# Running sums of weight tiles in a Strassen-type feed-forward block: accumulating DMAs instead of VectorE subtractions

## The chip, the cores and the metric

The kernel runs on one core of a Trainium2 chip. The metric is device time of one execution in microseconds, smaller is better. Before the change it takes 2362.85 us (median of three runs, 2361.63 to 2367.12).

## What is computed

The reference is one layer of an encoder for two sequences of 256 tokens (512 columns in all), width 2048, everything in float32:

```python
h = h + concat(neighbourhood_attention(xn), gated_deltanet_bidir(xn)) @ w_out   # xn = rmsnorm(h) @ w_in
hn = rmsnorm(h, norm_ffn_w)
h = h + (silu(hn @ w_gate) * (hn @ w_up)) @ w_down      # 2048 -> 5632 -> 2048
y = rmsnorm(h, final_norm_w)
```

The change touches only `hn @ w_gate` and `hn @ w_up`, and the preparation of their moving operand.

## The kernel before, in words

**Precision.** TensorE multiplies in fp32r. Every float32 operand is split into a high part (ScalarE rounds it, line 123) and a low part (VectorE subtracts the high part from the operand, line 124), and one product is three matmuls: high by high, high by low, low by high. A 128x1024 weight tile thus costs one ScalarE instruction and one VectorE instruction before its last matmuls can start. High and low tiles have three buffers each (`w_split`, line 874), so splits can run at most three products ahead of TensorE.

**The gate and up blocks.** `block` (line 883) computes two 128-column strips of gate or up for all 512 columns. The contraction (2048 = 2 x 1024) and the columns (two halves of 256) and the strips make a 2x2 by 2x2 block product, done in Winograd's form of Strassen's scheme: seven products instead of eight. Each `product` (line 866) is 24 matmuls of 256 columns. The moving operands, seven combinations of the four quarters of the normalised residual (A11, A12, S4, A22, S1, S2, S3), are made once ahead of the stage (lines 844 to 857) and kept in SBUF. The weight side needs seven operands for each block: four raw 512 KB tiles (b11, b12, b21, b22, loaded from HBM on the SP queue, lines 888 to 893) and combinations of them, which VectorE makes in place (lines 905, 909, 915, 927). Evacuation of the seven products to the four output quarters is a handful of ScalarE copies and VectorE additions.

There are 22 pairs of one gate and one up block, 44 blocks in all, in the loop at the end of the stage. b11 and b12 have one buffer in the gate pool and one in the up pool, so the two kinds of block alternate between them; b21 and b22 share a ring of three buffers with the other weight loads.

**What orders the work.** TensorE's matmuls keep program order. On the other engines a scheduler lists the instructions by priority; splits are written under `tc.high_priority(offset=AHEAD)` (120) and loads under three times that, which puts them ahead of their place in the program. Each engine and each DMA-issuing queue then runs its list strictly in order, waiting on semaphores. DMAs are issued from SP (weight loads) and from POOL (stores of the residual, line 843; stores of each pair's activations to `s_act`, line 971; their reload, line 995).

After the stage, the activations are reloaded for the down projection (`load_act`, line 990), whose loads are plain 512 KB DMAs issued from POOL into a ring of two buffers.

Of the kernel before, what the change touches and what calls it, by code (L numbers as in the profile page):

```python
# [8 lines left out]
F32 = mybir.dt.float32  # L9
# [3 lines left out]
ALU = mybir.AluOpType  # L13
# [4 lines left out]
P = 128  # L18
# [5 lines left out]
L = 256  # L24
# [34 lines left out]
def hybrid_encoder(ctx: ExitStack, tc: tile.TileContext, xT, w_in, w_ba, w_out, w_gate,  # L59
                   w_up, w_down, nw_mix, nw_ffn, nw_fin, na_bias, conv_w, lane_par,  # L60
                   dn_nw, y):
    nc = tc.nc
    act = nc.scalar.activation
    tt = nc.vector.tensor_tensor
# [5 lines left out]
    def mm(*a, **k):  # L70
        pin(nc.tensor.matmul(*a, **k))  # L71
# [6 lines left out]
    wp = ctx.enter_context(tc.tile_pool(name="wp", bufs=2, side="left"))  # L78
# [41 lines left out]
    def split(hi, lo, src, scale=None):  # L120

        if scale is None:
            act(out=hi, in_=src, func=AF.Copy)  # L123
            tt(lo, src, r32(hi), ALU.subtract)  # L124
# [710 lines left out]
    A11, A12, S4, A22, S1, S2, S3 = range(7)  # L835
    for n, i in enumerate(pairs):
        j = i % 8
        ps = pg.tile([P, T], F32, tag="g", name="ps_g")
        hk = st.tile([P, T], F32, tag="hk", bufs=2, name="hk")
        nc.sync.dma_start(hk, s_h1[i])  # L840
        half_gemm(ps, w_out[i, 1], dns, True, True)
        tt(hk, hk, ps, ALU.add)
        nc.gpsimd.dma_start(s_h2[i], hk)
        w = nwf[:, i:i + 1]
        if i < 8:
            cmb = st.tile([P, 7, L], F32, tag="cmb", name="cmb")
            a21 = st.tile([P, L], F32, tag="a21", name="a21")
            act(out=cmb[:, A11], in_=hk[:, :L], func=AF.Copy, scale=w)
            act(out=a21, in_=hk[:, L:], func=AF.Copy, scale=w)
            tt(cmb[:, S3], cmb[:, A11], a21, ALU.subtract)  # L850
        else:
            act(out=cmb[:, A12], in_=hk[:, :L], func=AF.Copy, scale=w)
            act(out=cmb[:, A22], in_=hk[:, L:], func=AF.Copy, scale=w)
            tt(cmb[:, S1], a21, cmb[:, A22], ALU.add)
            tt(cmb[:, S2], cmb[:, S1], cmb[:, A11], ALU.subtract)
            tt(cmb[:, S4], cmb[:, A12], cmb[:, S2], ALU.subtract)
            split(XH[j], XL[j], cmb)
        sq = acc if n == 0 else st.tile([P, T], F32, tag="sq", name="h_sq")
        act(out=sq, in_=hk, func=AF.Square)
        if n:  # L860
            tt(acc, acc, sq, ALU.add)
# [4 lines left out]
    def product(ps, w, c, first, done=False):  # L866

        wh, wl = w
        for k in range(8):
            for n, (u, x) in enumerate(((wh, XH), (wh, XL), (wl, XH))):  # L870
                mm(ps, u[:, k], x[k][:, c], start=(first and k == 0 and n == 0),
                   stop=(done and k == 7 and n == 2), skip_group_check=True)

    def w_split(src):
        hi = wp.tile([P, 8, P], F32R, tag="hi", bufs=3, name="w_hi")
        lo = wp.tile([P, 8, P], F32R, tag="lo", bufs=3, name="w_lo")
        split(hi, lo, src)
        return hi, lo

    def ahead():  # L880
        return tc.high_priority(offset=AHEAD)

    def block(src, f, pool, new_out, opened=None):

        with tc.high_priority(offset=3 * AHEAD):
            b11 = pool.tile([P, 8, P], F32, tag="b11", name="b11")
            b12 = pool.tile([P, 8, P], F32, tag="b12", name="b12")
            nc.sync.dma_start(b11, src[f, 0])
            nc.sync.dma_start(b12, src[f + 1, 0])
            b22 = wp.tile([P, 8, P], F32, tag="raw", bufs=3, name="b22")  # L890
            nc.sync.dma_start(b22, src[f + 1, 1])
            b21 = wp.tile([P, 8, P], F32, tag="raw", bufs=3, name="b21")
            nc.sync.dma_start(b21, src[f, 1])
        pa = pg.tile([P, T], F32, tag="g", name="ps_a")
        pc = psm.tile([P, T], F32, tag="s", name="ps_c")
        with ahead():
            w = w_split(b11)
        product(pa[:, :L], w, A11, True)
        if opened:
            opened()  # L900
        fp, out = state["fp"], new_out()
        p1 = fp.tile([P, L], F32, tag="p1", bufs=2, name="p1")
        nc.scalar.copy(p1, pa[:, :L])
        with ahead():
            tt(b11, b12, b11, ALU.subtract)
            w = w_split(b11)
        product(pc[:, L:], w, S1, True)
        with ahead():
            tt(b12, b22, b12, ALU.subtract)
            w = w_split(b12)  # L910
        product(pc[:, :L], w, S3, False)
        p75 = fp.tile([P, 2, L], F32, tag="p75", bufs=2, name="p75")
        nc.scalar.copy(p75, pc.rearrange("p (a t) -> p a t", a=2))
        with ahead():
            tt(b11, b22, b11, ALU.subtract)
            w = w_split(b11)
        product(pa[:, L:], w, S2, False)
        u2 = fp.tile([P, L], F32, tag="u2", bufs=2, name="u2")
        tt(u2, p1, pa[:, L:], ALU.add)
        with ahead():  # L920
            w = w_split(b22)
        product(pc[:, L:], w, S4, False, True)
        v = fp.tile([P, L], F32, tag="v", name="v")
        tt(v, u2, p75[:, 0], ALU.add)
        tt(out[:, 3], v, p75[:, 1], ALU.add)
        with ahead():
            tt(b11, b21, b11, ALU.subtract)
            w = w_split(b11)
        product(pc[:, :L], w, A22, False, True)
        with ahead():  # L930
            w = w_split(b21)
        tt(out[:, 1:3], pc.rearrange("p (a t) -> p a t", a=2),
           u2[:, None, :].broadcast_to([P, 2, L]), ALU.add)
        product(pa[:, :L], w, A12, False, True)
        nc.scalar.copy(out[:, 0], pa[:, :L])
# [20 lines left out]
    for p in range(NPAIR):  # L956
        g4 = block(w_gate, 2 * p, gA,
                   lambda: state["fp"].tile([P, 4, L], F32, tag="g4", name="ga"),
                   open_gate if p == 0 else None)
        act(out=g4, in_=g4, func=AF.Silu)  # L960
        u4 = block(w_up, 2 * p, state["gB"],
                   lambda: state["fp"].tile([P, 4, L], F32, tag="u4", bufs=2, name="up"))
        tt(u4, u4, g4, ALU.mult)  # L963
        sA = state["sA"]
        if p // 2 == FIRST_SEG:
            k = p % 2 * 2
            split(sA[:, 0, k:k + 2].rearrange("p k t -> p (k t)"),
                  sA[:, 1, k:k + 2].rearrange("p k t -> p (k t)"),
                  u4.rearrange("p a t -> p (a t)"))
        else:  # L970
            nc.gpsimd.dma_start(s_act[p], u4.rearrange("p a t -> p (a t)"))  # L971
# [16 lines left out]
    fp = ctx.enter_context(tc.tile_pool(name="fq", bufs=2, side="left", reuse_waits="tile"))  # L988
# [174 lines left out]
```

## Time and profile before

| | |
|---|---|
| median of the runs | 2362.85 us |
| the profiled execution's own time | 2364.33 us |
| its span, first to last instruction | 2362.6 us |
| TensorE busy | 2323.2 us, 98% |
| VectorE busy | 1599.0 us, 68% |
| ScalarE busy | 975.0 us, 41% |
| mean granted TensorE clock | 0.996 |
| gate and up stage, first matmul to the last block's last copy | 965.5 to 1864.8 us |

A busy share is an average over stages with different limits. Matmuls overlap each other in the pipeline, so their busy times are added up from a modelled end; the distance between starts is the better measure. The rows of the stage are shown where the prediction uses them.

### The profile page before, as it was taken

To read this page: it belongs to the slowest core of one execution; us is meant where nothing else is said; L and a number is where in the kernel's file an instruction comes from. 1 tells how busy PE (TensorE), PEld (TensorE's weight loads), DVE (VectorE), ACT (ScalarE), POOL (GpSimd) and SP (SyncE) were. 2 spreads that over 40 slices of the span, in tenths; PEclk is the share of its full clock that TensorE was granted. 3 is DMA by queue.
4 is the path that set the end of the run, shared out by engine and by line. 5 is a ranking of instruction groups with operands and counts; after the bars stand their busy time and mean duration, and the time that the engine had idled before them with its cause. 6 is when DMAs were issued, how large, how long until landed. Compare 5 with 4: busy or idle time off the path is not lost.

```text
span 2362.6 us, 35608 instructions
## 1 busy us (share of the span) xinstructions
PE 2323.2 (98%) x14500; PEld 2058.6 (87%) x14500; DVE 1599.0 (68%) x2164; ACT 975.0 (41%) x1464; POOL 143.8 (6%) x244
## 2 busy tenths in 40 slices
PE   8999999999999999899999999999999999999997
PEld 6777788877778788799999999999999888888887
DVE  7644699985566637788888888888888653422346
ACT  6777223324333315544444444444444331211125
POOL 2111200002100001000000000000000110000000
PEclk9999999999999999999999999999999999999999
DMA  5434623346434546333333333333333563423332
GB/s 202 130 116 132 161 93 103 95 120 179 145 115 125 212 157 208 120 115 119 116 126 117 126 117 119 114 121 113 118 106 99 192 227 98 133 93 97 98 125 72
DMA packets 88980, 305.30 MB, mean 129 GB/s; under 512 B 11776, under 2 KB 16288, under 8 KB 87664
## 3 DMA queue, kind: packets, MB, share of 16 engines
q1 hardware_dynamic: 71392, 245.67, 32.5%
q0 software_dynamic: 17424, 57.36, 8.0%
q8 instruction: 114, 1.87, 0.3%
q14 instruction: 50, 0.41, 0.1%
HBM read 266.98 MB, written 36.00 MB: 128 GB/s over the span
## 4 chain that ended last, share of the span: by engine, by line
PE 57%; DVE 0%; DMA 0%; issue 0%; ACT 0%; POOL 0%; DVEq 0%
PE ps_c L71 21%; PE ps_a L71 16%; PE ps_g L71 11%; PE ps_s L71 9%; DMA raw_a<-s_act 0%; DVE hT L1043 0%; DVE w_lo L124 0%; DVE up L937 0%; ACT w_hi L123 0%; ACT aq L123 0%; DVE up L963 0%; DVE hT L1010 0%; DVE dgs L1037 0%; POOL s_act L971 0%; DVE ssq_acc L1060 0%
## 5 line engine op out<-in xcount | busy, mean ns | idle before, releaser
L123 ACT ACTIVATE w_hi<-b 128x1024 fp32r<-128x1024 f32 x308 | 327.0, 1062 | 490.9 <-PE ps_c L71 164.6
L124 DVE TENSOR_TENSOR w_lo<-w_raw,w_hi 128x1024 fp32r<-128x1024 f32 x224 | 274.1, 1224 | 277.9 <-ACT w_hi L123 273.9
L124 DVE TENSOR_TENSOR w_lo<-b,w_hi 128x1024 fp32r<-128x1024 f32 x308 | 376.3, 1222 | 120.3 <-ACT w_hi L123 120.3
L123 ACT ACTIVATE w_hi<-w_raw 128x1024 fp32r<-128x1024 f32 x224 | 236.8, 1058 | 487.0 <-PE ps_s L71 278.2
L71 PE MATMUL ps_c<-xch,w_hi 128*128 128x256 f32 x1408 | 399.9, 284 | 0.0
L71 PE MATMUL ps_c<-xcl,w_hi 128*128 128x256 f32 x1408 | 399.0, 283 | 0.0
L71 PE MATMUL ps_c<-xch,w_lo 128*128 128x256 f32 x1408 | 399.0, 283 | 0.0
L71 PE MATMUL ps_g<-xhi,w_hi 128*128 128x512 f32 x896 | 369.6, 412 | 0.0
L71 PE MATMUL ps_g<-xhi,w_lo 128*128 128x512 f32 x896 | 351.6, 392 | 6.6 <-DVE w_lo L124 6.6
L71 PE MATMUL ps_g<-xlo,w_hi 128*128 128x512 f32 x896 | 350.8, 392 | 0.0
L71 PE MATMUL ps_a<-xch,w_hi 128*128 128x256 f32 x1056 | 299.0, 283 | 5.3 <-ACT xch L123 4.0
L71 PE MATMUL ps_a<-xcl,w_hi 128*128 128x256 f32 x1056 | 299.1, 283 | 1.7 <-DVE xcl L124 1.7
L71 PE MATMUL ps_a<-xch,w_lo 128*128 128x256 f32 x1056 | 299.0, 283 | 0.0
L71 PEld LDWEIGHTS ps_c<-xch,w_hi 128*128 128x128 f32 x1408 | 271.0, 192 | 0.5 <-issue 0.5
L71 PEld LDWEIGHTS ps_c<-xcl,w_hi 128*128 128x128 f32 x1408 | 271.0, 192 | 0.5 <-issue 0.5
L71 PEld LDWEIGHTS ps_c<-xch,w_lo 128*128 128x128 f32 x1408 | 270.9, 192 | 0.0
L71 PEld LDWEIGHTS ps_g<-xhi,w_lo 128*128 128x128 f32 x896 | 168.8, 188 | 46.0 <-DVE w_lo L124 9.1
L71 PEld LDWEIGHTS ps_a<-xch,w_hi 128*128 128x128 f32 x1056 | 202.7, 192 | 5.7 <-ACT xch L123 4.2
L71 PEld LDWEIGHTS ps_g<-xhi,w_hi 128*128 128x128 f32 x896 | 169.0, 189 | 43.1 <-issue 7.4
L71 PEld LDWEIGHTS ps_a<-xcl,w_hi 128*128 128x128 f32 x1056 | 202.8, 192 | 1.9 <-DVE xcl L124 1.9
L71 PEld LDWEIGHTS ps_a<-xch,w_lo 128*128 128x128 f32 x1056 | 202.9, 192 | 0.0
L71 PEld LDWEIGHTS ps_g<-xlo,w_hi 128*128 128x128 f32 x896 | 169.3, 189 | 30.9 <-issue 0.2
(307 smaller groups left out, 3468.7 us busy)
## 6 DMA issues: line engine op xcount, KB each, us to landing
w_raw<-in_w_in_dram SPq DMA_DIRECT2D x112, 512.0 KB, 3.6
b<-in_w_gate_dram SPq DMA_DIRECT2D x88, 512.0 KB, 3.5
b<-in_w_up_dram SPq DMA_DIRECT2D x88, 512.0 KB, 3.5
w_raw<-in_w_down_dram SPq DMA_DIRECT2D x88, 512.0 KB, 3.5
w_raw<-in_w_out_dram SPq DMA_DIRECT2D x32, 512.0 KB, 3.6
s_act<-up POOLq DMA_DIRECT2D x20, 512.0 KB, 2.9
raw_a<-s_act POOLq DMA_DIRECT2D x20, 512.0 KB, 4.6
qg<-s_eg SPq DMA_DIRECT2D x8, 1024.0 KB, 4.6
```

The source lines that it names most:

```text
L71: pin(nc.tensor.matmul(*a, **k))
L123: act(out=hi, in_=src, func=AF.Copy)
L124: tt(lo, src, r32(hi), ALU.subtract)
```

## The change

The weight operands become running sums. Two tiles replace b11 and b12 (here B11, B12, B21, B22 are the four raw tiles):

- `second` is loaded with B12 and then receives B22 by an accumulating DMA; it is used once.
- `first` is loaded with B11, used, receives B12, is used again, receives B22, is used again, receives B21, and is used a last time. Each addition is a DMA of 512 KB from HBM with `accum_op=ALU.add`, issued from POOL, into the same SBUF buffer.

The four VectorE subtractions of a block go. Signs that they carried move to the combinations of the residual (lines 854 and 856: S1 becomes a difference, S4 a sum) and to the evacuation. The order of the seven products changes, and the evacuation with it: ScalarE copies p1, p7 and one output quarter; VectorE does d, u2, three output quarters one by one, and the scaling. Line numbers on the plus side are those of the changed kernel.

```diff
-            tt(cmb[:, S1], a21, cmb[:, A22], ALU.add)
+            tt(cmb[:, S1], a21, cmb[:, A22], ALU.subtract)
             tt(cmb[:, S2], cmb[:, S1], cmb[:, A11], ALU.subtract)
-            tt(cmb[:, S4], cmb[:, A12], cmb[:, S2], ALU.subtract)
+            tt(cmb[:, S4], cmb[:, A12], cmb[:, S2], ALU.add)
...
+    def plus(dst, src):
+        nc.gpsimd.dma_start(dst, src, accum_op=ALU.add)
...
         with tc.high_priority(offset=3 * AHEAD):
-            b11 = pool.tile([P, 8, P], F32, tag="b11", name="b11")
-            b12 = pool.tile([P, 8, P], F32, tag="b12", name="b12")
-            nc.sync.dma_start(b11, src[f, 0])
-            nc.sync.dma_start(b12, src[f + 1, 0])
+            first = pool.tile([P, 8, P], F32, tag="first", name="w_first")
+            nc.sync.dma_start(first, src[f, 0])
+            second = pool.tile([P, 8, P], F32, tag="second", name="w_second")
+            nc.sync.dma_start(second, src[f + 1, 0])
+            plus(second, src[f + 1, 1])
...
         with ahead():
-            w = w_split(b11)
+            w = w_split(first)
+            plus(first, src[f + 1, 0])
         product(pa[:, :L], w, A11, True)
...
         with ahead():
-            tt(b11, b12, b11, ALU.subtract)
-            w = w_split(b11)
-        product(pc[:, L:], w, S1, True)
+            w = w_split(second)
+        product(pc[:, :L], w, S3, True)
+        p7 = fp.tile([P, L], F32, tag="p7", bufs=2, name="p7")
+        nc.scalar.copy(p7, pc[:, :L])
         with ahead():
-            tt(b12, b22, b12, ALU.subtract)
-            w = w_split(b12)
-        product(pc[:, :L], w, S3, False)
-        p75 = fp.tile([P, 2, L], F32, tag="p75", bufs=2, name="p75")
-        nc.scalar.copy(p75, pc.rearrange("p (a t) -> p a t", a=2))
+            w = w_split(first)
+            plus(first, src[f + 1, 1])
+        product(pc[:, L:], w, S1, False)
+        d = fp.tile([P, L], F32, tag="d", bufs=2, name="d")
+        tt(d, pc[:, L:], p7, ALU.subtract)
         with ahead():
-            tt(b11, b22, b11, ALU.subtract)
-            w = w_split(b11)
-        product(pa[:, L:], w, S2, False)
+            w = w_split(b21)
+        product(pa[:, :L], w, A12, False)
+        nc.scalar.copy(out[:, 0], pa[:, :L])
+        with ahead():
+            w = w_split(first)
+            plus(first, src[f, 1])
+        product(pa[:, L:], w, S2, False, True)
         u2 = fp.tile([P, L], F32, tag="u2", bufs=2, name="u2")
         tt(u2, p1, pa[:, L:], ALU.add)
+        tt(out[:, 3], d, u2, ALU.subtract)
         with ahead():
             w = w_split(b22)
-        product(pc[:, L:], w, S4, False, True)
...
+        product(pc[:, L:], w, S4, False)
+        tt(out[:, 2], pc[:, L:], u2, ALU.subtract)
         with ahead():
-            tt(b11, b21, b11, ALU.subtract)
-            w = w_split(b11)
+            w = w_split(first)
         product(pc[:, :L], w, A22, False, True)
...
-        product(pa[:, :L], w, A12, False, True)
-        nc.scalar.copy(out[:, 0], pa[:, :L])
+        tt(out[:, 1], pc[:, :L], u2, ALU.add)
```

More of the change, by code (lines that the diff above doesn't have):

```diff
@@ L881, in ahead @@
         return tc.high_priority(offset=AHEAD)
+    def plus(dst, src):
+        nc.gpsimd.dma_start(dst, src, accum_op=ALU.add)
     def block(src, f, pool, new_out, opened=None):
         with tc.high_priority(offset=3 * AHEAD):
-            b11 = pool.tile([P, 8, P], F32, tag="b11", name="b11")
-            b12 = pool.tile([P, 8, P], F32, tag="b12", name="b12")
-            nc.sync.dma_start(b11, src[f, 0])
-            nc.sync.dma_start(b12, src[f + 1, 0])
+            first = pool.tile([P, 8, P], F32, tag="first", name="w_first")
[3 more added lines that the diff above has]
+            plus(second, src[f + 1, 1])
+            b21 = wp.tile([P, 8, P], F32, tag="raw", bufs=3, name="b21")
+            nc.sync.dma_start(b21, src[f, 1])
             b22 = wp.tile([P, 8, P], F32, tag="raw", bufs=3, name="b22")
             nc.sync.dma_start(b22, src[f + 1, 1])
-            b21 = wp.tile([P, 8, P], F32, tag="raw", bufs=3, name="b21")
-            nc.sync.dma_start(b21, src[f, 1])
         pa = pg.tile([P, T], F32, tag="g", name="ps_a")
@@ L904, in block @@
         with ahead():
-            tt(b11, b12, b11, ALU.subtract)
-            w = w_split(b11)
-        product(pc[:, L:], w, S1, True)
+            w = w_split(second)
+        product(pc[:, :L], w, S3, True)
+        p7 = fp.tile([P, L], F32, tag="p7", bufs=2, name="p7")
+        nc.scalar.copy(p7, pc[:, :L])
         with ahead():
-            tt(b12, b22, b12, ALU.subtract)
-            w = w_split(b12)
-        product(pc[:, :L], w, S3, False)
-        p75 = fp.tile([P, 2, L], F32, tag="p75", bufs=2, name="p75")
-        nc.scalar.copy(p75, pc.rearrange("p (a t) -> p a t", a=2))
-        with ahead():
-            tt(b11, b22, b11, ALU.subtract)
-            w = w_split(b11)
-        product(pa[:, L:], w, S2, False)
+            w = w_split(first)
[3 more added lines that the diff above has]
+        tt(d, pc[:, L:], p7, ALU.subtract)
+        with ahead():
+            w = w_split(b21)
[5 more added lines that the diff above has]
+        product(pa[:, L:], w, S2, False, True)
         u2 = fp.tile([P, L], F32, tag="u2", bufs=2, name="u2")
         tt(u2, p1, pa[:, L:], ALU.add)
+        tt(out[:, 3], d, u2, ALU.subtract)
         with ahead():
             w = w_split(b22)
-        product(pc[:, L:], w, S4, False, True)
-        v = fp.tile([P, L], F32, tag="v", name="v")
-        tt(v, u2, p75[:, 0], ALU.add)
-        tt(out[:, 3], v, p75[:, 1], ALU.add)
+        product(pc[:, L:], w, S4, False)
+        tt(out[:, 2], pc[:, L:], u2, ALU.subtract)
         with ahead():
-            tt(b11, b21, b11, ALU.subtract)
-            w = w_split(b11)
+            w = w_split(first)
         product(pc[:, :L], w, A22, False, True)
[L930 to L933, printed above, removed]
-        product(pa[:, :L], w, A12, False, True)
-        nc.scalar.copy(out[:, 0], pa[:, :L])
+        tt(out[:, 1], pc[:, :L], u2, ALU.add)
         a = out.rearrange("p (f b) t -> p f (b t)", f=2)
```

## Prediction

> **What bounds the kernel now.** I read the page first, then the stage that the change touches by stretches of time, then that stage's tiles and steps.
>
> ```profile
> span 2362.6 us, 35608 instructions
> ...
> PE 2323.2 (98%) x14500; PEld 2058.6 (87%) x14500; DVE 1599.0 (68%) x2164; ACT 975.0 (41%) x1464; POOL 143.8 (6%) x244
> ...
> DVE  7644699985566637788888888888888653422346
> ...
> PE 57%; DVE 0%; DMA 0%; issue 0%; ACT 0%; POOL 0%; DVEq 0%
> ```
>
> TensorE is busy 98% of the span, and the chain of work that ended last holds no VectorE time. VectorE's row stands at 7 and 8 tenths from slice 17 to slice 31, the gate and up stage. Within that stage, in busy us and instruction counts of each engine (PE, PEld, DVE, ACT, POOL), clock, DMA share and GB/s:
>
> ```profile
> 1100.00:1800.00 700.00, 700.00 (x5835) 700.00 (x5835) 575.06 (x576) 312.34 (x366) 8.53 (x16) 1.00 0.37 118
> ```
>
> TensorE and its weight loads are busy for all 700 us at full clock: 700/5835 = 0.120 us per matmul, 24 x 0.120 = 2.88 us per product. VectorE is at 82% and waits for others; it is not the limit. The tile ps_a gives the pace (minimum, median and maximum ns, first and last start):
>
> ```profile
> L71 PEld LDWEIGHTS ps_a<-xch,w_hi x1056: 186/192/192, 965.5 to 1863.3; 128*128 128x128 f32 x176
> L919 DVE TENSOR_TENSOR u<-p,ps_a x44: 420/422/422, 988.5 to 1855.3; 128x256 f32<-128x256 f32 x44
> L935 ACT COPY ga<-ps_a x22: 353/353/354, 998.0 to 1844.7; 128x256 f32<-128x256 f32 x22
> ```
>
> u is made once a block, so a block takes (1855.3 - 988.5)/43 = 20.16 us, which is 7 x 2.88. The first block takes 998.0 - 965.5 = 32.5 us because it waits for the moving operands. So the stage is TensorE's, and anything that shortens VectorE's list is worth nothing there unless TensorE has something to wait for.
>
> **What the change removes.** Groups of the stage by line, with busy us and mean ns:
>
> ```profile
> L927 DVE TENSOR_TENSOR b<-b,b 128x1024 f32<-128x1024 f32 x43 | 52.6, 1224 | 0.8
> L905 DVE TENSOR_TENSOR b<-b,b 128x1024 f32<-128x1024 f32 x42 | 51.5, 1226 | 1.4
> L915 DVE TENSOR_TENSOR b<-b,b 128x1024 f32<-128x1024 f32 x42 | 51.4, 1225 | 1.4
> L909 DVE TENSOR_TENSOR b<-b,b 128x1024 f32<-128x1024 f32 x42 | 51.1, 1216 | 0.0
> ```
>
> 44 x 4 = 176 VectorE instructions of 1.22 us go, 215 us of busy time, all beside a TensorE that never waits: worth 0 in the steady stage. The evacuation has one VectorE instruction more a block (d, u2, three quarters, scaling, against u2, v, two writes, scaling) and ScalarE as many as before: 0. The signs in the residual's combinations change no count: 0. The number of matmuls is the same: 0.
>
> **What it adds.** 176 accumulating DMAs of 512 KB, issued from POOL. Those into `second` have a block's time of lead and I cost them as traffic only. Those into `first` lie in a chain. The same buffer is split, added to, split, added to, split, added to, split: product 3's weights can't be copied by ScalarE before the addition has landed, the addition can't be issued before VectorE's low part of product 1 has read the tile, and so on. Three additions in a block. The next block has its own buffer, but the instruction order of the changed kernel puts its first split behind this block's last on both engines: on ScalarE the copies of products 7, 1', 2' (prime: next block) follow each other, on VectorE the low part of 7 is followed by u2, the out[:, 3] subtraction, and the low part of 1'. So the chains of consecutive blocks don't overlap. A block then takes
>
> P = 3 X + 3 S + E,
>
> if that is over 20.16, with X from the end of one low part to the start of ScalarE's copy of the sum, S from that start to the end of the next low part, and E from the low part of product 7 to that of product 1'. S and E come from steps in the timeline (start, duration):
>
> ```profile
> 1509.62 1.06 ACT L123 ACTIVATE w_hi<-b 128x1024 fp32r<-128x1024 f32 x1 [1.82 <-PE ps_c L71]
> ```
> ```profile
> 1510.72 1.23 DVE L124 TENSOR_TENSOR w_lo<-b,w_hi 128x1024 fp32r<-128x1024 f32 x1 [1.03 <-ACT w_hi L123]
> 1512.58 0.42 DVE L919 TENSOR_TENSOR u<-p,ps_a 128x256 f32<-128x256 f32 x1 [0.63 <-PE ps_a L71]
> 1513.10 0.43 DVE L924 TENSOR_TENSOR v<-u,p 128x256 f32<-128x256 f32 x1
> 1513.56 0.43 DVE L925 TENSOR_TENSOR ga<-v,p 128x256 f32<-128x256 f32 x1
> 1513.91 1.22 DVE L124 TENSOR_TENSOR w_lo<-b,w_hi 128x1024 fp32r<-128x1024 f32 x1
> 1516.43 1.23 DVE L124 TENSOR_TENSOR w_lo<-b,w_hi 128x1024 fp32r<-128x1024 f32 x1 [1.30 <-ACT w_hi L123]
> 1517.69 1.23 DVE L905 TENSOR_TENSOR b<-b,b 128x1024 f32<-128x1024 f32 x1
> ```
>
> S = 1510.72 + 1.23 - 1509.62 = 2.33. For E: a small instruction behind a low part starts about when that ends; then u2 to the next 0.52 (1513.10 - 1512.58), small to low part 0.35 (1513.91 - 1513.56), low part 1.22: 2.09. So P = 3 X + 6.99 + 2.09 = 3 X + 9.08, and it exceeds TensorE's 20.16 from X = 3.69 on.
>
> No row of before shows an accumulation. The nearest is the plain 512 KB load that POOL issues in the down stage, into a ring whose buffer VectorE's low part has just freed, and which ScalarE then waits for: the same loop.
>
> ```profile
> 1915.94 1.23 DVE L124 TENSOR_TENSOR ar<-raw_a,ar 128x1024 fp32r<-128x1024 f32 x1 [1.13 <-ACT ar L123]
> 1922.23 1.23 DVE L124 TENSOR_TENSOR ar<-raw_a,ar 128x1024 fp32r<-128x1024 f32 x1 [1.44 <-ACT ar L123]
> ```
> ```profile
> 1917.46 0.53 POOL L995 DMA_DIRECT2D raw_a<-s_act  x1 [2.42 <-DVE ar L124]
> 1923.76 0.53 POOL L995 DMA_DIRECT2D raw_a<-s_act  x1 [2.13 <-DVE ar L124]
> ```
> ```profile
> 1921.14 1.06 ACT L123 ACTIVATE ar<-raw_a 128x1024 fp32r<-128x1024 f32 x1 [1.60 <-DMA raw_a<-s_act]
> 1928.58 1.06 ACT L123 ACTIVATE ar<-raw_a 128x1024 fp32r<-128x1024 f32 x1 [1.90 <-DMA raw_a<-s_act]
> ```
> ```profile
> DMA to landing us min/median/max: 3.7/4.6/11.8
> ```
>
> X of a plain load: 1921.14 - 1917.17 = 3.97, and 1928.58 - 1923.46 = 5.12 in a stretch with other loads. The smallest landing, 3.7, and the 0.29 from VectorE's end to POOL's issue give 3.99 too. An accumulation also reads its destination. What 512 KB cost the engines, from 700 us of the stage:
>
> ```profile
> q1 hardware_dynamic: 20115, 73.29, 33.5%
> q0 software_dynamic: 2304, 8.39, 3.0%
> ...
> b<-in_w_gate_dram SPq DMA_DIRECT2D x71, 512.0 KB, 3.5
> b<-in_w_up_dram SPq DMA_DIRECT2D x69, 512.0 KB, 3.5
> s_act<-up POOLq DMA_DIRECT2D x16, 512.0 KB, 2.9
> ```
>
> 140 loads in 0.335 x 700 = 234.5 us of all 16 engines: 1.67 us each; a store 0.03 x 700/16 = 1.3. The second read adds between 0 (if it runs beside the first) and 1.67 (if behind it). I take 1.67, since the engine has to move twice the bytes in: X = 5.64 undisturbed. Then contention: a block's other traffic is four loads (6.7), the accumulation into `second` (3.3) and half a store (0.7), 10.7 us in a period near 28, 38%. An addition that meets a load may lose up to its 1.67; 0.38 x 1.67 = 0.65. I take X = 6.3; the ends are 3.97 (nothing for the second read, nothing met) and 5.12 + 2 x 1.67 = 8.46.
>
> On what only a page states: the Trainium skill, "Collectives: The Full Stack", section "The bandwidth ceiling", says that an addition in the DMA engine is free but takes two source reads on one ring, so that it moves at half a copy's rate. By that X would be 5.64 before contention and the time 2364 + 43 x (26.00 - 20.16) = 2615; no run so far shows an accumulation.
>
> **The sum.** P = 3 x 6.3 + 9.08 = 27.98, 7.82 us over 20.16. The first block's 32.5 us cover its own chain, so 43 blocks pay: 336 us. On the profiled execution's own 2364.33 (1.5 above the median of the runs): 2364 + 336 = 2700.
>
> **Waits and queues.** Behind ScalarE's waiting copy for product 3 stand the copy for 4, p1 and p7; none is needed before product 3 has run, so they add nothing. POOL holds the accumulation into the next same-kind `second` between the first and second addition to `first`; it waits for a load that SP issues after the low part of product 2, 1.57 us after that of product 1 (0.35 and 1.22), landing 3.5 us later: 5.1 us into the block. The second addition is ready at X + 2.33 = 8.6, later, so it isn't held; it would be only if that load were over 3 us late. SP's order of loads follows the splits that free their buffers, and each lands a block early. The `s_act` store stands ahead of the third addition and is ready by then. In the residual stage before, stores on POOL now stand behind the first accumulation into `second`: a few us at most, and in the first block three VectorE sums go ahead of the last moving operands, up to 3.7 us the other way. I cost both at 0.
>
> **The rivals.**
>
> - *The accumulation costs hardly more than a plain load.* X 3.97 to 5.1; for it speaks that the second read is from SBUF and might hide in the 2 us of a landing that isn't transfer (3.7 - 1.67); against it the doubled bytes. At X = 4.5: P = 22.58, 43 x 2.42 = 104, 2468 us.
> - *Every addition meets another transfer and queues.* The splits release loads and additions at the same moments, so the meetings aren't random: X 7.3 to 8.5. At 8.0: P = 33.08, 43 x 12.92 = 556, 2920 us. Against it: the DMA share is only 0.37 now.
> - *Not slower: the chain fits under TensorE.* The place is the loop above, and it decides at X = 3.69. Below that, TensorE stays the bound: 2364, or some 3.7 us less from the shorter first block, 2361. Against it: the smallest X seen for a plain load is 3.97. The Trainium skill, "DMA: Bandwidth & Descriptors", section "Anatomy of one DMA", gives 2.0 us plus the bytes at 436 GB/s, 3.2 us for 512 KB; by that X would be 3.5 and nothing would change. The trace disagrees, at 3.7 for the fastest of 20.
> - *The sums stay where they were.* The instruction order of the changed kernel has 176 more DMAs on POOL and 132 fewer instructions of two tensors on VectorE (176 sums less, 44 evacuations more), so this doesn't happen: chance 0.
>
> **How the numbers follow.** Forecast (X 5.1 to 7.3, 2546 to 2829): 0.53. Plain-like accumulation (X 3.73 to 5.1, up to 2546): 0.22. Queued accumulation (X over 7.3): 0.19. Fits under TensorE: 0.06, of which 0.02 faster. A measurement of this kernel tells 0.2%, some 4.7 us, from no change; the chain passes that at X = 3.73. So faster 0.02, same 0.04, slower 0.94. The range 2430 (X = 4.2) to 2950 (X = 8.24) leaves out the last case, a little of the plain-like case and half of the queued one, under 2 in 10.
>
> **What would show it.** Right: TensorE in the stage no longer at 100%, with three waits a block, ahead of products 3, 5 and 7, near 2, 3 and 3 us, released by the low part and behind it by the DMA into w_first; block period near 28; landing of these DMAs near 6 us; ScalarE's copy waiting on DMA. Wrong: a period that isn't 3 X + 9.1 with the X seen (another wait closes the loop); waits on `second` or on the loads; POOL's issue of additions held behind another DMA; or a period of 20.16.

## The result and the profile after

The changed kernel takes 2746.99 us (median of four runs, 2739.04 to 2754.95) against 2363.91 (four runs, 2361.63 to 2367.12): 1.1619 times as long, with a 95% interval of 1.1582 to 1.1657. The prediction said 2700, slower. The profiled execution took 2739.04 us, 374.7 more than that of before.

From the page of the changed kernel: the span, the engines, then VectorE's, the clock's and the DMA engines' rows of the 40 slices.

```profile
span 2737.3 us, 35744 instructions
...
PE 2447.2 (89%) x14500; PEld 2158.2 (79%) x14500; DVE 1396.0 (51%) x2032; ACT 954.3 (35%) x1464; POOL 297.7 (11%) x420
...
DVE  7544999756663754443443444443444455342246
...
PEclk9999999999999998999999989989999899999999
DMA  5336233554455667666666666666666656342332
```

VectorE does 203 us less, as the removal of 176 sums and the 44 added evacuations promise, and its row falls from 7 and 8 to 3 and 4 in the stage. The whole gets longer all the same. The same stretch of the stage as before, with the same columns (busy us of PE, PEld, DVE, ACT, POOL, then clock, DMA share and GB/s), and the packets of the two queues in it:

```profile
1100.00:1800.00 700.00, 553.44 (x4022) 539.52 (x4021) 284.90 (x324) 203.71 (x252) 90.15 (x108) 0.90 0.64 153
```
```profile
q0 software_dynamic: 15437, 56.16, 43.4%
q1 hardware_dynamic: 13823, 50.33, 19.9%
```

TensorE is busy 79% where it was busy throughout, does 4022 matmuls where it did 5835, and is granted 0.90 of its clock. Nothing else is near full: the DMA engines are at 0.64, VectorE at 41%, ScalarE at 29%. Where no engine is full, a chain of waits is the place to look. The stage's pace, from the tile that is made once a block:

```profile
L931 DVE TENSOR_TENSOR u<-p,ps_a x44: 412/414/422, 992.6 to 2234.2; 128x256 f32<-128x256 f32 x44
```

(2234.2 - 992.6)/43 = 28.87 us a block against 20.16. Over 43 blocks that is 1241.6 - 866.8 = 374.8: the whole difference is in this stage. The waits in it (1200 to 2100 us; total, times, longest):

```profile
POOL w_first L885 <- DVE w_lo L124: 574.8, 77, 11.5
DVE w_lo L124 <- ACT w_hi L123: 400.1, 88, 9.2
ACT w_hi L123 <- DMA w_first<-in_w_gate_dram: 231.7, 40, 9.7
ACT w_hi L123 <- DMA w_first<-in_w_up_dram: 213.8, 37, 9.8
...
POOL w_second L885 <- DMA w_second<-in_w_gate_dram: 83.9, 13, 7.6
POOL w_second L885 <- DMA w_second<-in_w_up_dram: 81.5, 13, 7.6
PE ps_c L71 <- DVE ga L936: 64.2, 16, 4.5
...
PE ps_c L71 <- DVE up L936: 56.5, 15, 5.6
...
PE ps_c L71 <- ACT p L915: 14.3, 31, 0.5
```

The first four rows are a circle: POOL waits for VectorE's low part, VectorE for ScalarE's high part, ScalarE for the DMA that POOL issued. One block of it, in the timeline of POOL, ScalarE and VectorE (start, duration):

```profile
1518.72 0.87 POOL L885 DMA_DIRECT2D w_first<-in_w_up_dram  x1 [8.91 <-DVE w_lo L124]
1526.06 0.87 POOL L885 DMA_DIRECT2D w_second<-in_w_up_dram  x1 [6.48 <-DVE ga L942]
1527.43 0.87 POOL L885 DMA_DIRECT2D w_first<-in_w_up_dram  x1 [0.51 <-DVE w_lo L124]
1537.74 0.87 POOL L885 DMA_DIRECT2D w_first<-in_w_up_dram  x1 [9.44 <-DVE w_lo L124]
```
```profile
1524.36 1.06 ACT L123 ACTIVATE w_hi<-w_first 128x1024 fp32r<-128x1024 f32 x1 [7.23 <-PE ps_c L71]
...
1535.13 1.06 ACT L123 ACTIVATE w_hi<-w_first 128x1024 fp32r<-128x1024 f32 x1 [4.69 <-DMA w_first<-in_w_up_dram]
...
1544.30 2.00 ACT L123 ACTIVATE w_hi<-w_first 128x1024 fp32r<-128x1024 f32 x2 [6.90 <-DMA w_first<-in_w_up_dram]
```
```profile
1517.20 1.22 DVE L124 TENSOR_TENSOR w_lo<-w_first,w_hi 128x1024 fp32r<-128x1024 f32 x1
...
1524.78 1.23 DVE L942 TENSOR_TENSOR ga<-ga,rstd 128x1024 f32<-128x1024 f32 x1
1525.92 1.22 DVE L124 TENSOR_TENSOR w_lo<-w_first,w_hi 128x1024 fp32r<-128x1024 f32 x1
...
1536.22 1.22 DVE L124 TENSOR_TENSOR w_lo<-w_first,w_hi 128x1024 fp32r<-128x1024 f32 x1 [6.79 <-ACT w_hi L123]
...
1545.38 1.23 DVE L124 TENSOR_TENSOR w_lo<-w_first,w_hi 128x1024 fp32r<-128x1024 f32 x1 [6.47 <-ACT w_hi L123]
...
1547.32 1.22 DVE L124 TENSOR_TENSOR w_lo<-w_first,w_hi 128x1024 fp32r<-128x1024 f32 x1
1548.45 0.42 DVE L936 TENSOR_TENSOR up<-ps_c,u 128x256 f32<-128x256 f32 x1
```

Product 1's low part ends at 1518.42. X1 = 1524.36 - 1518.42 = 5.94; S1 = 1527.14 - 1524.36 = 2.78; X2 = 1535.13 - 1527.14 = 7.99; S2 = 2.31; X3 = 1544.30 - 1537.44 = 6.86; S3 = 2.31; E = 1548.54 - 1546.61 = 1.93. Read so over 41 blocks, the means are X 6.01, 8.09 and 5.71 (together 6.60), S 2.61, 2.31, 2.31, E 1.93. Their sum is 28.97, and the tile above says 28.87. That the two agree shows little: the terms follow each other from one low part to the next, so they add up to the period whatever holds a block up. What speaks for the chain is in the terms. S and E, 9.16 together, are about as long as the 9.08 worked out without a wait; the additions are issued 0.29 us (median) after the low part before them; and the copies for products 5 and 7 waited last for the DMA in all 41 blocks, those for product 3 in 21 (19 times product 7 came later).

### The profile page after: what moved, and what is told of

It is laid out like the page before. It is cut to its first block, busy times and chain, and to the rows that moved or that the text cites. A ratio compares the mean times of both kernels' runs of the same rounds, so it can differ in the third digit from the quotient of the medians.

```text
span 2737.3 us, 35744 instructions
## 1 busy us (share of the span) xinstructions
PE 2447.2 (89%) x14500; PEld 2158.2 (79%) x14500; DVE 1396.0 (51%) x2032; ACT 954.3 (35%) x1464; POOL 297.7 (11%) x420
## 5 line engine op out<-in xcount | busy, mean ns | idle before, releaser
L71 PE MATMUL ps_c<-xch,w_hi 128*128 128x256 f32 x1408 | 443.6, 315 | 184.0 <-DVE up L936 82.1
L124 DVE TENSOR_TENSOR w_lo<-w_first,w_hi 128x1024 fp32r<-128x1024 f32 x176 | 215.2, 1223 | 538.2 <-ACT w_hi L123 530.8
L71 PEld LDWEIGHTS ps_c<-xch,w_hi 128*128 128x128 f32 x1408 | 305.8, 217 | 201.1 <-issue 168.0
L123 ACT ACTIVATE w_hi<-w_first 128x1024 fp32r<-128x1024 f32 x176 | 181.6, 1054 | 771.8 <-DMA w_first<-in_w_up_dram 329.3
L71 PE MATMUL ps_c<-xcl,w_hi 128*128 128x256 f32 x1408 | 433.5, 308 | 0.0
L71 PE MATMUL ps_c<-xch,w_lo 128*128 128x256 f32 x1408 | 432.5, 307 | 0.0
L71 PE MATMUL ps_a<-xch,w_hi 128*128 128x256 f32 x1056 | 312.0, 295 | 74.6 <-ACT up L925 37.9
L71 PEld LDWEIGHTS ps_c<-xcl,w_hi 128*128 128x128 f32 x1408 | 306.9, 218 | 0.5 <-issue 0.5
L71 PEld LDWEIGHTS ps_c<-xch,w_lo 128*128 128x128 f32 x1408 | 306.5, 218 | 0.0
L71 PEld LDWEIGHTS ps_a<-xch,w_hi 128*128 128x128 f32 x1056 | 212.0, 201 | 83.8 <-ACT up L925 42.4
```

## The experiments

The theory is the prediction's: the period of a block is the sum of three X, three S and E, and X is long because an accumulation moves twice the bytes and meets other transfers. The rivals are two: the new order of the evacuation makes TensorE wait (the profile after names line 936 ahead of product 7); the added traffic itself slows the stage. X, S and E of an experiment are means over its blocks, read from the timeline as above. Where no interval stands, a single execution was timed.

### VectorE makes the sums into `first` again

The order of products and the evacuation of the changed kernel stay; B12 is loaded once more as a raw tile.

```diff
+            b12 = wp.tile([P, 8, P], F32, tag="raw", bufs=3, name="b12")
+            nc.sync.dma_start(b12, src[f + 1, 0])
...
-            plus(first, src[f + 1, 0])
+            tt(first, first, b12, ALU.add)
...
-            plus(first, src[f + 1, 1])
+            tt(first, first, b22, ALU.add)
...
-            plus(first, src[f, 1])
+            tt(first, first, b21, ALU.add)
```

> The changed kernel's order of products, signs and evacuation, with second still summed by an accumulating DMA, but the three sums into first made by VectorE from raw tiles (B12 gets a load of its own). Chain theory (the period of 28.9 us is three additions by DMA in series, three splits of 2.3 and 1.9 us to the next block): with no DMA in the chain the period returns to TensorE's 20.16, time 2355 to 2375. Rival, evacuation and TensorE (product 7 can't start before the out[:, 2] instruction has read its bank, and runs at half clock after the wait): order and evacuation are unchanged, so most of the loss stays, over 2550. Rival, DMA traffic: less traffic too (5 plain loads and 1 accumulation a block), so 2355 to 2450; it isn't told apart here.

Measured: 2558.45 us, 1.0815 times before (1.0797 to 1.0834). The rival hits: without any addition by DMA in a chain, the new order and evacuation cost 194 us, (2055.0 - 994.7)/43 = 24.66 a block. Its tile row, and the waits of TensorE from 1200 to 2000 us:

```profile
L933 DVE TENSOR_TENSOR u<-p,ps_a x44: 421/422/422, 994.7 to 2055.0; 128x256 f32<-128x256 f32 x44
```
```profile
PE ps_c L71 <- ACT p L917: 44.2, 33, 1.3
PE ps_a L71 <- ACT up L927: 21.4, 16, 1.3
PE ps_a L71 <- ACT ga L927: 21.4, 16, 1.3
PE ps_c L71 <- DVE up L938: 16.9, 16, 1.1
PE ps_c L71 <- DVE ga L938: 16.9, 16, 1.1
```

Three times a block TensorE waits for a read of the other half of the accumulator that it is about to write: product 3 writes the right half of ps_c and waits for the copy of its left half into p7, and so on. Part of each wait is the order of instructions in this kernel: on ScalarE a copy of weights of 1.06 us, which the end of the same product releases, runs ahead of the copy into p7. In the changed kernel, where that copy runs at once, product 3 waits 0.46 us for it (14.3 us in 31 times). In the kernel before, a product into the other accumulator lies between such a read and the next write. The trace cannot say whether this loss and the chain's add up in the changed kernel, or lie beside each other.

### Four accumulators, with sums by VectorE and by DMA

Two kernels. Products 3 and 6 get an accumulator pd of their own, product 5 gets pb; one kernel is the one just told, the other is the changed kernel.

```diff
+        pb = pg.tile([P, T], F32, tag="g", name="ps_b")
+        pd = psm.tile([P, T], F32, tag="s", name="ps_d")
...
-        product(pc[:, L:], w, S1, False)
+        product(pd[:, L:], w, S1, True)
...
-        product(pa[:, L:], w, S2, False, True)
+        product(pb[:, L:], w, S2, True, True)
...
-        product(pc[:, L:], w, S4, False)
+        product(pd[:, L:], w, S4, False, True)
```

With the sums by VectorE:

> The kernel with VectorE's sums into first (period 24.66), with four PSUM banks a block in the same way. Theory: its whole loss of 4.5 us a block is TensorE waiting for p7, out[:, 0] and out[:, 2] to be read from the other half of the bank it writes next; without these waits 2355 to 2380. Rival, the order of the splits on ScalarE and VectorE, with sums in the chain of the splits, is the cause: little changes, over 2500.

Measured: 2363.17 us, 0.9996 times before (0.9986 to 1.0006). In its stretch from 1200 to 1800 us TensorE is busy throughout, at full clock:

```profile
1200.00:1800.00 600.00, 600.00 (x5003) 600.00 (x5002) 470.69 (x493) 262.08 (x316) 33.38 (x43) 1.00 0.61 169
```

So the whole loss of the kernel before it was these waits. It also shows that the accumulation into `second`, which is kept here and has a block's lead, costs nothing in this kernel. With the sums by DMA:

> The changed kernel with products 3 and 6 and product 5 written to PSUM tiles of their own (four banks a block instead of two), so that no product waits for the evacuation of the other half of its bank. Chain theory (the period is 3 additions, 3 splits and 1.9): the chain stays; only the first addition loses the wait for the late product 7 (6.0 to 5.7, its split 2.6 to 2.3), period 28.4, time 2700 to 2735. Rival, waits for the evacuation in the same bank are the cause (4.5 us a block where VectorE made the sums): 2747 - 43 x 4.5 = 2553 or less.

Measured: 2794.22 us, 1.1812 (1.1785 to 1.1839), slower than the changed kernel. That was not expected by any theory. The waits for evacuations are gone from TensorE's list, and X has grown to 6.58, 9.23 and 6.37 (E is 1.16):

```profile
L933 DVE TENSOR_TENSOR u<-p,ps_b x44: 414/421/423, 990.4 to 2289.0; 128x256 f32<-128x256 f32 x44
```

Period 30.2; the sum of the terms is 22.18 + 6.93 + 1.16 = 30.27. Taking TensorE's waits for evacuations away gives nothing back here, so they seem to lie beside the chain in the changed kernel; since X moved too, the clean comparison is that of the two kernels without the accumulation into `second`, below. The two kernels of this section differ in who makes the sums into `first`: by VectorE the time is 2363.17 us, by DMA 2794.22. What made the additions slower is the subject of a later run.

### Additions made plain loads

This kernel loads without adding, so the products use single raw tiles in place of the sums.

```diff
-        nc.gpsimd.dma_start(dst, src, accum_op=ALU.add)
+        nc.gpsimd.dma_start(dst, src)
```

> The changed kernel with the four additions made plain loads from POOL into the same buffers at the same places (the weights are then not summed). Chain theory: the wait from low part to ScalarE's copy falls from 6.0, 8.1 and 5.7 to about 4.3, 5.2 and 4.0, period 22.6, time 2440 to 2510; the second read of the destination is then about half of the loss. Rival, DMA traffic: 8 units instead of 12 a block, 19.3 us a block at the changed kernel's rate, so about 2364. Rival, evacuation and TensorE: little changes, over 2650.

Measured: 2517.53 us, just over the expected range, and with each X 0.3 to 0.4 longer than expected. X 4.70, 5.63, 4.27, S 2.53, 2.31, 2.31, E 1.97, sum 23.72; the tile gives (2013.3 - 995.1)/43 = 23.68.

```profile
L931 DVE TENSOR_TENSOR u<-p,ps_a x44: 411/414/422, 995.1 to 2013.3; 128x256 f32<-128x256 f32 x44
```
```profile
w_first<-in_w_gate_dram POOLq DMA_DIRECT2D x66, 512.0 KB, 3.9
```

The changed kernel's page has 5.4 us in this row:

```profile
w_first<-in_w_gate_dram POOLq DMA_DIRECT2D x66, 512.0 KB, 5.4
```

Landing falls from 5.4 to 3.9 us and X from a mean of 6.60 to 4.87. Of the 8.7 us that a block lost, 5.2 come from the additions being additions; 3.5 would be lost to the same circle with plain loads.

### No accumulation into `second`

One of the seven weight operands is then B12 alone.

```diff
-            plus(second, src[f + 1, 1])
```

> The changed kernel without the accumulation into second (S3's weights then lack B22). Chain theory: only the second addition to first gets shorter, since the accumulation into second stands right ahead of it in POOL's queue: 8.1 to about 5.8, period 26.6, time 2620 to 2670. Rival, DMA traffic: 10 units instead of 12, period 24, about 2530. Rival, evacuation and TensorE: over 2700.

Measured: 2653.78 us. X 6.04, 5.81, 5.97: the second addition falls from 8.09 to 5.81 and the others stay. Period 26.84, (2149.5 - 995.4)/43:

```profile
L930 DVE TENSOR_TENSOR u<-p,ps_a x44: 411/414/422, 995.4 to 2149.5; 128x256 f32<-128x256 f32 x44
```

So about 2 us of each block are a meeting of two accumulations. In the block shown, the one into `second` is issued at 1526.06 and the second one into `first` at 1527.43. The changed kernel's own trace shows it as well, block by block: where the two issues lie 1.1 us apart or less (17 of 41 blocks), the second X is 8.9 to 10.2; where they lie 1.5 to 2.4 apart (12 blocks), 6.4 to 7.2; in the 3 blocks with more between them, 5.7 to 6.1. The other 9 blocks lie in between.

### Traffic without a chain

Two kernels from the one before the change, each with accumulations into a spare buffer that nobody reads. In the first, three DMAs a block:

```diff
+            if "gB" in state:
+                spare = state["gB"].tile([P, 8, P], F32, tag="spare", name="w_spare")
+                nc.gpsimd.dma_start(spare, src[f, 0])
+                nc.gpsimd.dma_start(spare, src[f + 1, 0], accum_op=ALU.add)
+                nc.gpsimd.dma_start(spare, src[f + 1, 1], accum_op=ALU.add)
...
-        p1 = fp.tile([P, L], F32, tag="p1", bufs=2, name="p1")
+        p1 = fp.tile([P, L], F32, tag="p1", bufs=1, name="p1")
```

> The kernel before, with one plain load and two accumulating DMAs of 512 KB a block from POOL into a spare tile that nobody reads (and p1 with one buffer instead of two, to make room). Per block 5 plain loads and 2 accumulations; if an accumulation costs the DMA engines twice a load that is 9 units in 20.16 us, a higher rate than the changed kernel's 12 units in 28.9. Chain theory: nothing waits for these, 2355 to 2380, with a landing of the accumulations of 5 to 6 us. Rival, DMA traffic: the loads of the block come late, over 2450. Rival, evacuation and TensorE: 2364.

Measured: 2607.00 us, 1.1020 (1.1003 to 1.1036). The rival, DMA traffic, had forecast over 2450, but the run says nothing of traffic. The scheduler put the spare's DMAs far ahead on POOL, the store of the activations stood behind them, and VectorE waited for that store's buffer, nine times in 800 us:

```profile
DVE up L930 <- DMA s_act<-up: 243.2, 9, 33.8
```

In the second, the spare's two accumulations wait for a one-column copy of p1 into the spare, which ties them to their block:

```diff
+        spare = state["spare"]
+        nc.scalar.copy(spare[:, 0, :1], p1[:, :1])
+        for i in range(2):
+            nc.gpsimd.dma_start(spare, src[f + i, 0], accum_op=ALU.add)
```

> The kernel before with two accumulating DMAs of 512 KB a block into a spare tile, released each block by p1 (a one-column copy), so that they run at the block's pace; nobody waits for the sums but the next one-column copy; p1 has one buffer. Traffic of 4 plain loads and 2 accumulations in 20.16 us, a DMA share near 0.6 as in the changed kernel. Chain theory: traffic of that size costs nothing where nobody waits, 2355 to 2380; landing of the accumulations 5 to 6 us. Rival, DMA traffic: loads come late, over 2420.

Measured: 2365.72 us, 1.0005 (0.9995 to 1.0014). The DMA share from 1200 to 1800 us is 0.66, above that of the changed kernel, and TensorE is busy throughout:

```profile
1200.00:1800.00 600.00, 600.00 (x5002) 600.00 (x5001) 492.77 (x494) 273.00 (x346) 59.56 (x73) 1.00 0.66 168
```
```profile
w_spare<-in_w_gate_dram POOLq DMA_DIRECT2D x44, 512.0 KB, 6.7
```

An accumulation may take 6.7 us (5 to 6 were expected) when nobody waits for it. Traffic at the rate of the changed kernel is not the cause by itself.

### The next block's first addition put ahead

From the kernel with four accumulators and sums by DMA: `block` is cut in two, so that the next block's loads, first split and first addition are written ahead of this block's last split.

```diff
-    def block(src, f, pool, new_out, opened=None):
+    def begin(src, f, pool):
...
+        return first, second, b21, b22, w
+
+    def block(src, f, tiles, new_out, nxt, opened=None):
...
+        after = nxt()
         with ahead():
             w = w_split(first)
         product(pc[:, :L], w, A22, False, True)
```

> The changed kernel with four banks a block and with the loads, the first split and the first addition of the next block put ahead of the last split of this block, so that the third addition of one block runs beside the first addition of the next. Chain theory: one X and one S leave the period: 28.4 - 5.7 - 2.3 + 1.2, about 21.6, up to 24 since two accumulations then share the queue and the DMA engines are busy 18.5 us a block: 2425 to 2530. Rival, DMA traffic (12 units of 1.5 to 1.7 us a block): the period cannot fall far, over 2600. Rival, waits in the bank: same as with four banks alone.

Measured: 2694.69 us, 1.1389 (1.1364 to 1.1414): 100 us less than the kernel it comes from, and far from the expected gain. Period (2188.8 - 994.0)/43 = 27.79. Its additions take 7.5 us to land, and the DMA share is 0.70:

```profile
1200.00:1800.00 600.00, 495.51 (x3585) 479.48 (x3584) 256.34 (x287) 183.66 (x225) 79.88 (x95) 0.89 0.70 160
```
```profile
w_first<-in_w_gate_dram POOLq DMA_DIRECT2D x66, 512.0 KB, 7.5
```

This is the time that the rival, DMA traffic, had forecast (over 2600). So the chain theory's forecast of what overlapping would win failed: landing goes from 5.4 to 7.5 us where additions of two blocks run beside each other, and POOL waits 153.7 us in 800 for the up blocks' load into `second` that its accumulation needs, with additions queued behind. Which of the two keeps the period near 28 was not separated.

### Four accumulators without the accumulation into `second`

This asks what made the additions slower in the kernel with four accumulators; one operand is again B12 alone.

```diff
-            plus(second, src[f + 1, 1])
```

> The kernel with four accumulators (in which the additions became slower than in the changed kernel, mean X 7.4) without the accumulation into second; one of the seven weight operands is then B12 alone. If that rise came from the accumulation into second, which stands ahead of an addition: X 5.7 to 6.0 in all three, period 26 to 26.8, 2610 to 2650 us. If it came from the loads of b21 and b22 and the store, whose places in the block moved: X of the first and third addition stay at 6.4 to 6.6 and only the second falls, to 6.5, period 27.8 to 28.3, 2690 to 2715 us.

Measured: 2650.06 us; X 5.97, 5.85, 6.23 (medians 5.86, 5.78, 5.81), period (2147.4 - 990.9)/43 = 26.90.

```profile
L932 DVE TENSOR_TENSOR u<-p,ps_b x44: 411/414/416, 990.9 to 2147.4; 128x256 f32<-128x256 f32 x44
```

With the accumulation into `second` gone, the rise is gone: two and four accumulators differ by 3.7 us in time (2653.78, 2650.06). So the rise came by way of that accumulation. It costs 3.3 us a block with four accumulators and 2.0 with two. The traces show most of what the second X gains by it: with four accumulators the two issues lie 1.1 us apart or less in 31 of 41 blocks, with two in 17. Why they come closer, and why the first and third X rise as well, stays open. The same pair is the clean test of the first rival: without these waits for evacuations the changed kernel's chain takes as long as with them.

### Additions of half the size

Two kernels in which each accumulation moves 256 KB, so that half of each sum is left out: from the changed kernel, and from the one with four accumulators.

```diff
-        nc.gpsimd.dma_start(dst, src, accum_op=ALU.add)
+        nc.gpsimd.dma_start(dst[:, :4], src[:, :4], accum_op=ALU.add)
```

> The changed kernel with each accumulation cut to half of its tile, 256 KB; half of each weight sum is left out, and every wait and the order of instructions stay. It asks whether X grows with the bytes that are moved or is a fixed price of an accumulation. If the second read's time is bytes (3.34 us of engine time for 512 KB in two reads, 1.67 for 256 KB, on 2.30 us that don't depend on size): undisturbed X 3.97, with less contention 4.2 to 4.7, period 21.7 to 23.2, 2430 to 2495 us. If an accumulation has a fixed surcharge of 1.7 us over a plain load, whatever its size: X 2.30 + 0.84 + 1.7 = 4.8 undisturbed, 5.0 to 5.5 with contention, period 24 to 25.6, 2530 to 2600 us. If X hardly depends on size (latency alone): near 6, 2650 us or more.

Measured: 2842.61 us, slower than with whole tiles, though the additions land sooner:

```profile
L931 DVE TENSOR_TENSOR u<-p,ps_a x44: 420/421/422, 991.2 to 2337.6; 128x256 f32<-128x256 f32 x44
```
```profile
w_first<-in_w_gate_dram POOLq DMA_DIRECT2D x66, 256.0 KB, 4.1
```

The scheduler has another order for them: on ScalarE the copy of p7 now stands behind the copy of product 5's weights, which waits for the second addition. TensorE waits for p7's copy before product 3. ScalarE's rows, then TensorE's:

```profile
1542.72 1.06 ACT L123 ACTIVATE w_hi<-w_first 128x1024 fp32r<-128x1024 f32 x1 [6.95 <-DMA w_first<-in_w_gate_dram]
1543.69 0.35 ACT L915 COPY p<-ps_c 128x256 f32<-128x256 f32 x1
```
```profile
1544.09 0.58 PE L71 MATMUL ps_c<-xch,w_hi 128*128 128x256 f32 x1 [6.67 <-ACT p L915]
```

The period is (2337.6 - 991.2)/43 = 31.31, of which three X (4.5, 8.3 and 6.9) leave 11.6 where S and E were worked out at 9.08. A new wait closes the loop, and the expectation, which took the order as given, missed. With four accumulators the copy stays ahead:

> The kernel with four accumulators, with each accumulation cut to half of its tile, 256 KB; half of each weight sum is left out. In its order of instructions ScalarE's copy of p7 stands ahead of its waiting copy of product 5's weights; in the kernel with halves and two accumulators it stood behind, and TensorE waited for it. If an accumulation's time grows with its bytes (undisturbed X 4.2 to 4.4, as the first addition showed there): the first and third X 4.2 to 4.8, the second, with second's accumulation ahead of it, 5.6 to 6.5, period 22.5 to 24.5, 2460 to 2550 us. If half an accumulation costs as much as a whole one plus or minus a little: X 6 to 9 as with whole tiles, period near 30, 2780 us. If another wait closes the loop: a period that isn't the sum of the three X, the three S and E.

Measured: 2606.16 us, over the expected 2550. X 4.47, 8.06, 4.48, S 2.31 each, E 1.94: 25.88, and the tile gives (2100.8 - 991.2)/43 = 25.80.

```profile
L933 DVE TENSOR_TENSOR u<-p,ps_b x44: 412/415/422, 991.2 to 2100.8; 128x256 f32<-128x256 f32 x44
```

The first and third X are as expected from bytes; the second missed by 2 us. In most blocks the accumulation into `second` is still issued right ahead of that addition, whose own issue is 0.73 us behind its low part on the mean (0.36 in the changed kernel); where they lie apart X is down to 4.41.

## Why the prediction was right

- **The chain** P = 3 X + 3 S + E: right. That the terms add up to the period is no test of it, since they follow each other. The test is whether the period less the three X measured stays at the 9.08 worked out for S and E, as the prediction asked. It does in the changed kernel (28.87 - 19.81 = 9.06), with plain loads (9.08), without the accumulation into `second` (9.02, and 8.85 with four accumulators) and with halves and four accumulators (8.79). With four accumulators and whole additions 8.0 are left, since E is 1.16 there. The two kernels that changed the order of instructions are the ones where another wait joins in (11.6 with halves and two accumulators; in the overlapped kernel the third X is gone from the chain).
- **X**: the size was off by a little. 6.60 on the mean against 6.3, which is 3 x 0.30 x 43 = 39 us, the distance from the forecast to the profiled execution. Undisturbed, X is 5.7 (the third addition) where 5.64 was worked out. But the two parts of that were not right one by one. Halving an addition takes 1.3 to 1.5 us off X (5.67 to 5.86 against 4.34 to 4.40, medians), so its bytes take 2.5 to 3.0 us where 3.34 was taken, if the time grows evenly with them, and 2.8 to 3.1 don't depend on size where 2.30 was taken. That the two errors cancel is luck. POOL's longer issue (0.87 us for an accumulation of either size, 0.53 for a plain load) may be 0.34 of the fixed part; no run separates it. The queues agree: in 700 us, q0's 0.434 x 700 = 304 us less 12 stores of 1.3 leave 288 for 96 accumulations, 3.0 each against 1.67 for a plain load. The Trainium skill's half rate ("Collectives: The Full Stack", section "The bandwidth ceiling") is near: measured is 1.67/3.0 = 0.56, or 0.48 against a load in the same stretch (0.199 x 700/96 = 1.45).
- **Contention** of 0.65 on every addition (0.38 x 1.67 is 0.63, which gives the same 6.3): mis-sized and in the wrong place. The mean X lies 0.9 over the undisturbed 5.7. Nearly all of it sits on the second addition, 8.09 against 5.7 to 6.0, because the accumulation into `second` runs beside it.
- **"So it isn't held"**: right for POOL's queue, wrong for the transfer. The second addition is issued 0.3 us (median) after its low part, as the others. But the load that `second` waits for lands in 5.5 us, not 3.5, beside the first addition (in 4.5 where VectorE makes the sums), so that its accumulation starts just ahead of the second addition and both are in flight together. The step looked at the order of issue and not at what is still moving.
- **S and E**: 7.23 and 1.93 against 6.99 and 2.09. S1 is longer because another instruction can stand ahead of the low part on VectorE (the scaling at 1524.78 in the block shown).
- **"The evacuation: 0"**: failed. It counted instructions and not who waits for them. With VectorE's sums the new evacuation costs 4.5 us a block, 8% of the time, because TensorE waits to write one half of an accumulator until the other half has been read. How much it costs depends on what stands ahead of the reads: with plain loads the whole period, chain and all, is 23.68, less than the 24.66 of that kernel. In the changed kernel this lies beside the longer chain, which hides it (without the accumulation into `second` the time is 2653.78 us with these waits and 2650.06 without them); that is luck of the forecast, not its reasoning. The Trainium skill ("Perfetto Trace Analysis", section "Matmuls") says that independent products should rotate through the accumulator's banks so that reads of one run beside the next product; the two runs with VectorE's sums agree, 24.66 us a block without it and TensorE full with it.
- **The waits that were to be seen**: landing near 6 (5.4), period near 28 (28.87) and ScalarE waiting on DMA came; three waits of 2, 3 and 3 us ahead of products 3, 5 and 7, ended by the low part, did not. The profile shows one ahead of product 7, 3.9 us on the mean and 5.6 at the longest, ended by line 936, and shorter ones ended by ScalarE's copies. Line 936 is the evacuation of product 6, but the chain holds it up: on VectorE it stands behind the low part of product 7 and three more instructions, and in the block shown it ends at 1548.87, 2.26 us after that low part. So the predicted wait is there and made longer by the evacuation, inside the time that the chain leaves free.
- **The rivals**: a plain-like addition would have given 2518 (measured, where 2468 was worked out from X = 4.5). Queueing is there, for one addition in three. That the chain fits under TensorE did not come near: even with plain loads the smallest X is 4.03, above 3.69.

No version here beats the kernel before: with the chain gone and four accumulators the time is 2363, for the stage is then TensorE's again, and VectorE's sums were never in its way.

## What to carry to other kernels

Before taking work off an engine that is not the bound, look at what the new place puts in a row: a DMA that lands in 5.4 us replaced an instruction of 1.22 us, three times in a row for each block, and no busy share shows that ahead of time; the sum of one round of the circle does. Follow reads of accumulators as well as their writers, and give products separate accumulators if they are to be read one by one. In an experiment that changes a size, look first at whether the order of instructions is still the same.

## What the runs showed of the hardware that was not expected

- After its longer waits TensorE's matmuls run at about half speed for a while. The first matmul of product 7 in the changed kernel, and one after an evacuation wait in the kernel with VectorE's sums, whose granted clock from 1200 to 1800 us is 1.00:

```profile
1518.90 0.55 PE L71 MATMUL ps_c<-xch,w_hi 128*128 128x256 f32 x1 [4.24 <-DVE ga L936]
```
```profile
1501.93 0.38 PE L71 MATMUL ps_c<-xch,w_hi 128*128 128x256 f32 x1 [1.34 <-ACT p L917]
```

  The changed kernel's trace has 40 stretches at half clock between 1100 and 2100 us, 3.4 or 6.8 us long and 198 us together; that is the granted clock of 0.90. Each begins in a wait of TensorE or within 1.4 us of its end. All 27 waits of 3.41 us or more have one, and so have 13 of the 15 between 2.6 and 3.4; none of 2.56 us or less has. Half speed makes product 7 late, and with it the copy of product 3's weights in 19 of 41 blocks, yet without product 7's wait for line 936 (four accumulators, no `second`) the time is the same within 4 us. The Trainium skill ("TensorE: Matmul & The Clock Gate", section "HAM oscillation — how this bites in real kernels") names idle gaps of more than about 3.4 us as the point from which the clock falls. The trace agrees for the waits above that, but 13 shorter ones, from 2.62 us, were enough too.
- POOL needs 0.87 us to issue an accumulation, of 512 or 256 KB, and 0.53 for a plain load of 512 KB (the rows of the timelines).
